# Feed-forward block products written as slots, each engine one step behind what it reads

## The chip, the cores and the metric

The kernel runs on one NeuronCore of one Trainium2 chip. The metric is the device time in microseconds (us) from start to end of one execution; where several runs are compared, their median.

## The reference

One decoder layer over 1024 tokens of width 1024: adaLN modulation, a mixer (sparse top-k attention of 8 heads beside a causal pooling), a LayerNorm, a SwiGLU feed-forward part of width 2816, a second LayerNorm. The change touches the feed-forward part alone:

```python
def swiglu(h, w_gate, w_up, w_down):
    return (jax.nn.silu(h @ w_gate) * (h @ w_up)) @ w_down
...
        h = x * (1.0 + scale2) + shift2
        ffn = swiglu(h, w_gate[l], w_up[l], w_down[l])
        x = layer_norm(ALPHA * x + gate2 * ffn, ln2_g[l], ln2_b[l])
```

## The kernel before

**Precision and splitting.** Every float32 operand of a matmul is kept as a high half (the value rounded to fp32r, written by ScalarE, ACT) and a low half (value less high half, a subtraction on VectorE, DVE, or GpSimd, POOL). A product of two blocks is then three matmuls: high by high, high by low, low by high.

**Tiling.** The 2816 feed-forward channels are cut into 11 pairs of 128-channel blocks (`NFP`), p = 0 to 10. For a pair the gate product, the up product and the down product are each a 2x2 by 2x2 block product done with seven block multiplications instead of eight (Strassen's scheme in Winograd's form). A **step** is one of the seven: 12 matmuls of 128x128 by 128x512 on TensorE (PE). I call the gate steps G1 to G7, the up steps U1 to U7 and the down steps D1 to D7, in the order of the tables `STEPS` and `DOWN`. G and U steps read the weight blocks A11, S3, S2, A12, S1, S4, A22 in that order, D steps the blocks B11, B21, T1, T4, T3, B22, T2. The names with S and T are sums or differences of quarters of the raw weights. Each D step also reads one block of activations: A11, A12, S1, A22, S3, S4, S2 for D1 to D7. In U the fourth step's twelve matmuls are halved, so that U4 has 6 and U5 has 18.

**Weights.** One megabyte of raw weights (four quarters of 128x512) is a set; two sets lie in SBUF (tiles `wraw_R` and `wraw_W`) and each is reloaded, on the SP queue, when its last block is made. POOL forms the sums and differences of quarters in place, for the down weights it first multiplies by the gate row `GR` ("gating", tile `gr`). ACT writes the block's high half, DVE (for down blocks POOL) its low half, into a ring of four blocks (tiles `wblk_V`, `wblk_T`). The function `make_block` issues all of this for one block at once, and `use_blocks` calls it after each step until `LEAD` = 4 blocks stand ahead of the next step.

**Results.** G and U steps accumulate in three PSUM banks (`gu`). G's results are combined on ACT and DVE and go through SiLU into `gtmp`; U's are combined in `utmp` and multiplied into `gtmp`. From the four products the seven activation blocks are made: A11, A12, A21 and A22 as they are or summed to S1, S2, S3, S4, each with a high half on ACT and a low half (tiles `act_W`, `act_R`). D steps go into four banks (`dn`), from which DVE adds into the residual stream (`res_X`), one addition of 128x512 per bank; the next D step writes the same four banks.

**Order.** From pair 1 on, the instructions of the four engines stay in the order in which the code issues them (`pinned`, through the `Queue` class); before and behind that a scheduler may move them. The table `DOWN_AT` interleaves a pair's G and U steps with the D steps of the pair before. Each step issues its matmuls, then its own combining, then the blocks to be made, then (`after_step`) low halves and sums put off from the step before. Every operation of all engines goes through the one helper that the profile shows as L159 (SP's as L156), so groups are told apart by their tiles.

The closing product (down weights of pairs 9 and 10, plain blocks), the residual and the second LayerNorm follow, 512 columns by 128 tokens at a time.

Of the kernel before, what the change touches and what calls it, by code (L numbers as in the profile page):

```python
# [171 lines left out]
def decoder_layer_kernel(  # L172
# [1149 lines left out]

    def make_block():
        if pos["made"] == len(blocks):
            return
        n_set, w_, end = blocks[pos["made"]]
        dst = block(pos["made"])
        pos["made"] += 1
        r = raw_set(n_set)
        a11, a12, a21, a22 = (r[:, q * 512 : (q + 1) * 512] for q in range(4))  # L1330
        if loads[n_set][0] == "d":
            gated = lambda x, c: G.tensor_tensor(x, x, GR[:, c * 512 : (c + 1) * 512], ALU.mult)
            if type(w_) is tuple:
                fi, c = w_
                src = r[:, fi * 1024 + c * 512 : fi * 1024 + (c + 1) * 512]
                gated(src, c)
            else:
                src = {"B11": a11, "B21": a21, "T1": a11, "T4": a21, "T3": a12, "B22": a22, "T2": a11}[w_]
                if w_ in ("B11", "B21"):
                    gated(src, 0)  # L1340
                elif w_ == "T1":
                    gated(a12, 1)
                    G.tensor_tensor(a11, a12, a11, ALU.subtract)
                elif w_ == "T4":
                    gated(a22, 1)
                    G.tensor_tensor(a11, a22, a11, ALU.subtract)
                    G.tensor_tensor(a21, a11, a21, ALU.subtract)
                elif w_ == "T3":
                    G.tensor_tensor(a12, a22, a12, ALU.subtract)
        else:  # L1350
            src = {"A11": a11, "S3": a11, "S2": a11, "A12": a12, "S1": a21, "A22": a22, "S4": a12}[w_]
            if w_ == "S3":
                G.tensor_tensor(a11, a11, a21, ALU.subtract)
            elif w_ == "S2":
                G.tensor_tensor(a11, a22, a11, ALU.subtract)
            elif w_ == "S1":
                G.tensor_tensor(a21, a21, a22, ALU.add)
            elif w_ == "S4":
                G.tensor_tensor(a12, a12, a11, ALU.subtract)
        split(dst, src, 512, G if loads[n_set][0] == "d" and type(w_) is str else V)  # L1360
        if end and n_set:
            load_set(n_set + 2)

    def use_blocks(n):
        pos["used"] += n

        lead = LEAD + 4 if pos["used"] >= len(blocks) - 11 else LEAD
        while pos["made"] < min(pos["used"] + lead, len(blocks)):
            make_block()

    def act_split(dst, s, j, eng):
        A.activation(dst[:, j], s[:, j], AF.Copy)
        eng.tensor_tensor(dst[:, 512 + j.start : 512 + j.stop], s[:, j], f_(dst[:, j]), ALU.subtract)

    gu_bank, gu_blk = {}, {}

    def gu_step(kind, n, i0, ni, act, halves=True):
# [18 lines left out]
        def out(q, val):

            s_ = GTMP[(0, 2, 1, 3)[q]]
            if kind == "g":
                A.activation(s_[:, j], val, AF.Silu)  # L1400
                return
            V.tensor_tensor(s_[:, j], s_[:, j], val, ALU.mult)
            if type(act) is list:
                act_split(act[q], s_, j, V)
                return
            g11, g12, g21, g22 = GTMP
            def act_hi(nm_, src):
                A.activation(act[nm_][:, j], src[:, j], AF.Copy)
                return lambda: (G if nm_ in ACT_G else V).tensor_tensor(
                    act[nm_][:, 512 + j.start : 512 + j.stop], src[:, j], f_(act[nm_][:, j]), ALU.subtract)  # L1410

            if q != 1:
                low.append(act_hi({0: "A11", 2: "A12", 3: "A22"}[q], s_))
            if q == 2:
                low.pop()()
            for nm_, dst, x, y, op in {1: (("S1", UTMP[0], g21, g22, ALU.add), ("S3", UTMP[2], g11, g21, ALU.subtract),
                                           ("S2", g11, UTMP[0], g11, ALU.subtract)),
                                       2: (("S4", g12, g11, g12, ALU.subtract),)}.get(q, ()):
                (G if nm_ in SUM_G else V).tensor_tensor(dst, x, y, op)
                if nm_ in SUM_G:  # L1420
# [265 lines left out]
```

## Time and profile before

| | |
|---|---|
| three runs | 1497.67, 1499.07, 1500.56 us; median 1499.07 |
| the profiled execution | 1506.66 us, of which the span of the profile is 1504.8 |
| TensorE, matmuls busy | 1267.5 us, 84% of the span |
| VectorE (DVE) busy | 1017.1 us, 68% |
| GpSimd (POOL) busy | 787.1 us, 52% |
| ScalarE (ACT) busy | 606.9 us, 40% |
| mean granted TensorE clock | 0.904 |

The span runs from the first to the last instruction; the execution's own time holds 1.9 us more, and profiled executions are timed apart from the three runs. Matmuls overlap, and a busy TensorE need not be at its full pace, so its share says little: how long a step of twelve takes says more. In the views, PE is TensorE's matmul queue and PEld its weight loads; a row `out<-in` names the tile written and those read; `[2.46 <-ACT gtmp_V]` is idle time ahead of the row and the instruction that ended it.

### The profile page before, as it was taken

The page shows a single profiled execution, that of the slowest core. Times are in us where ns is not written, and L with a number is a line of the kernel's source. Part 1 is how long each engine was busy: PE and PEld are TensorE (multiplying, and loading weights), DVE is VectorE, ACT ScalarE, POOL GpSimd, SP SyncE. Part 2 cuts the span into 40 slices and gives each one's busy share as a digit, 9 for nine tenths or more (in the row PEclk, how much of TensorE's full clock was granted, in tenths as well). Part 3 has the DMA queues.
Part 4 walks back from the last instruction along what each step waited for, and adds up shares of the span by engine and source line. Part 5 has one row for each costly group of instructions (what it writes and reads, how often), then busy time and mean ns, then how long its engine had stood idle before and what let it go on. Part 6 is the DMA issues. An engine that isn't in the chain of part 4 may idle for free.

```text
span 1504.8 us, 16018 instructions
## 1 busy us (share of the span) xinstructions
PE 1267.5 (84%) x5462; PEld 974.9 (65%) x5462; DVE 1017.1 (68%) x1740; ACT 606.9 (40%) x1141; POOL 787.1 (52%) x764
## 2 busy tenths in 40 slices
PE   7888978687699799966797979797979797979796
PEld 6655657565466458855675757575757575757675
DVE  6898898999877955885564646464646464646488
ACT  2456626446567662752232323232323232323331
POOL 1574856674243642466737373737373737272548
PEclk9999989897679989987898989898989898989998
DMA  9520113011003743011020202020202020202012
GB/s 346 208 99 15 53 39 112 29 42 35 14 15 107 237 157 124 1 42 42 28 84 0 84 0 84 1 84 0 84 1 84 1 84 0 84 0 84 28 56 112
DMA packets 24999, 101.80 MB, mean 68 GB/s; under 512 B 3411, under 2 KB 3411, under 8 KB 20566
## 3 DMA queue, kind: packets, MB, share of 16 engines
q1 hardware_dynamic: 24918, 100.78, 19.0%
q8 instruction: 43, 0.70, 0.2%
q14 instruction: 38, 0.31, 0.1%
HBM read 92.38 MB, written 8.40 MB: 67 GB/s over the span
## 4 chain that ended last, share of the span: by engine, by line
PE 21%; POOL 16%; DVE 6%; ACT 4%; issue 3%; DMA 1%; DVEq 0%; POOLq 0%; ACTq 0%; SPq 0%
PE gu L159 11%; PE dn L159 9%; POOL wraw_R L159 5%; POOL wraw_W L159 4%; POOL act_W L159 2%; POOL gtmp_V L159 2%; DVE act_W L159 1%; DVE gtmp_V L159 1%; ACT wblk_T L159 1%; ACT wblk_V L159 1%; POOL wblk_T L159 1%; POOL wblk_V L159 1%; DVE utmp_X L159 1%; ACT act_W L159 1%; POOL res_X L159 1%
## 5 line engine op out<-in xcount | busy, mean ns | idle before, releaser
L159 PE MATMUL gu<-hr_H,wblk_V 128*128 128x512 f32 (+1 forms) x936 | 229.1, 397 | 28.7 <-ACT gtmp_V L159 16.7
L159 PE MATMUL gu<-hr_H,wblk_T 128*128 128x512 f32 (+1 forms) x924 | 228.3, 402 | 23.3 <-ACT gtmp_V L159 20.1
L159 PEld LDWEIGHTS gu<-hr_H,wblk_V 128*128 128x128 f32 x936 | 180.3, 197 | 69.8 <-ACT gtmp_V L159 20.0
L159 PEld LDWEIGHTS gu<-hr_H,wblk_T 128*128 128x128 f32 x924 | 180.5, 201 | 63.8 <-ACT gtmp_V L159 23.6
L159 DVE TENSOR_TENSOR res_X<-res_X,dn 128x512 f32<-128x512 f32 (+1 forms) x253 | 156.9, 676 | 1.8 <-PE dn L159 1.8
L159 POOL TENSOR_TENSOR wraw_R<-wraw_R 128x512 f32<-128x512 f32 x64 | 86.1, 1348 | 107.6 <-DVE wblk_V L159 57.0
L159 PE MATMUL pj<-ws_W,hT_H 128*128 128x512 f32 x456 | 125.9, 426 | 18.9 <-DVE kr_K L159 6.5
L159 POOL TENSOR_TENSOR wraw_W<-wraw_W 128x512 f32<-128x512 f32 x60 | 79.3, 1326 | 92.1 <-DVE wblk_T L159 51.3
L159 PEld LDWEIGHTS pj<-ws_W,hT_H 128*128 128x128 f32 x456 | 89.8, 203 | 47.0 <-issue 16.8
L159 PE MATMUL dn<-wblk_T,act_W 128*128 128x512 f32 x324 | 94.8, 447 | 23.7 <-ACT wblk_T L159 14.3
L159 PE MATMUL dn<-wblk_V,act_W 128*128 128x512 f32 x324 | 94.7, 447 | 22.8 <-ACT wblk_V L159 14.3
L159 PEld LDWEIGHTS dn<-wblk_T,act_W 128*128 128x128 f32 x324 | 69.3, 217 | 45.4 <-ACT wblk_T L159 16.0
L159 PEld LDWEIGHTS dn<-wblk_V,act_W 128*128 128x128 f32 x324 | 69.4, 217 | 43.9 <-ACT wblk_V L159 16.0
L159 POOL TENSOR_SCALAR sm_H<-sm_H,stat_X 128x1024 f32<-128x1024 f32 (+7 forms) x64 | 58.4, 925 | 75.2 <-DVE stat_X L159 62.1
L159 DVE TENSOR_TENSOR wblk_V<-wraw_W,wblk_V 128x512 fp32r<-128x512 f32 x40 | 32.4, 810 | 78.0 <-ACT wblk_V L159 78.0
L159 DVE TENSOR_TENSOR wblk_V<-wraw_R,wblk_V 128x512 fp32r<-128x512 f32 x38 | 30.4, 800 | 80.7 <-ACT wblk_V L159 77.7
L159 DVE TENSOR_TENSOR wblk_T<-wraw_W,wblk_T 128x512 fp32r<-128x512 f32 x41 | 32.9, 805 | 76.8 <-ACT wblk_T L159 76.8
L159 DVE TENSOR_SCALAR_CACHE_REDUCE junk_X<-keysD_T,colsD_X 128x1024 int16<-128x1024 int16 (+1 forms) x64 | 79.0, 1270 | 0.8
L159 ACT ACTIVATE wblk_V<-wraw_R 128x512 fp32r<-128x512 f32 x56 | 35.1, 628 | 97.5 <-POOL wraw_R L159 71.0
L159 DVE TENSOR_TENSOR wblk_T<-wraw_R,wblk_T 128x512 fp32r<-128x512 f32 x36 | 28.8, 805 | 64.2 <-ACT wblk_T L159 64.1
L159 ACT ACTIVATE wblk_V<-wraw_W 128x512 fp32r<-128x512 f32 x54 | 33.9, 627 | 79.3 <-POOL wraw_W L159 63.3
L159 ACT ACTIVATE wblk_T<-wraw_W 128x512 fp32r<-128x512 f32 x55 | 34.3, 625 | 74.6 <-POOL wraw_W L159 60.0
(299 smaller groups left out, 2814.8 us busy)
## 6 DMA issues: line engine op xcount, KB each, us to landing
wm_K<-in_wma_dram SPq DMA_DIRECT2D x16, 512.0 KB, 8.9
modraw_V<-in_wmc_dram SPq DMA_DIRECT2D x16, 512.0 KB, 4.4
wraw_R<-in_wg_dram SPq DMA_DIRECT2D x6, 1024.0 KB, 4.8
wraw_R<-in_wd_dram SPq DMA_DIRECT2D x6, 1024.0 KB, 4.7
wraw_W<-in_wup_dram SPq DMA_DIRECT2D x6, 1024.0 KB, 4.7
modraw_V<-in_wmg_dram SPq DMA_DIRECT2D x10, 512.0 KB, 4.5
wraw_R<-in_wup_dram SPq DMA_DIRECT2D x5, 1024.0 KB, 4.8
wraw_W<-in_wg_dram SPq DMA_DIRECT2D x5, 1024.0 KB, 4.9
```

The costliest lines, as they stand in the source:

```text
L159: ins_ = f(*a, **k)
```

## The change

The steps' arithmetic is the same, and so are the matmuls of each. Four things differ.

1. **Slots.** `gu_step` and `down_step` issue only their matmuls and return a `Slot` with four parts: `copy` (ACT's copy of the step's own bank, or the four residual additions of a D step), `vec` (DVE's combining), `sums`, and `act` (ACT's SiLU or high halves of activations). `slot(sl)` then issues, behind the matmuls of this step: the `vec` of the step before, the low halves whose high halves were issued a slot ago, the `sums` of the step before, POOL's preparation, up to two high halves of weights, pending high halves of activations, the `act` of the step before, and last this step's `copy`.
2. **Weights.** `make_block` is cut into `block_prep` (POOL's sums and gating), `block_high` (ACT) and `block_low` (DVE or POOL). High halves reach up to `may_make()`, preparation one block further, as far as `may_prep()` finds that no quarter is overwritten that a later low half reads. Two halves of a set are reloaded apart: one behind S4's low half, one behind the last block's.
3. **Order.** `DOWN_AT` is new: a pair now runs G1 G2 D1 G3 D2 G4 G5 D3 G6 G7 D4 D5 U1 D6 U2 U3 D7 U4 U5 U6 U7, where it ran G1 G2 D1 G3 D2 G4 D3 G5 D4 G6 D5 G7 D6 U1 D7 U2 to U7.
4. **Who does what.** Only S4's low half of the activations and the sum S3 stay on POOL; the low halves of S2 and S3 and the sums S2 and S4 are on DVE. Before the last pair, POOL's eight additions on the residual stream stood in a row; now they stand behind single steps of that pair. Pair 0's G steps and their blocks are issued `at_once`, as before.

```diff
-LEAD = 4
-ACT_G = ("S2", "S3", "S4")
-SUM_G = ("S2", "S3", "S4")
-DOWN_AT = "ggdgdgdgdgdgduduuuuuu"
+ACT_G = ("S4",)
+DOWN_AT = "ggdgdggdggdduduuduuuu"
...
+    def block_prep():
+        n = pos["prep"]
+        pos["prep"] += 1
+        for st in steps_of(n):
+            if type(st) is int:
+                x = quad(n, st)
+                G.tensor_tensor(x, x, GR[:, st % 2 * 512 : (st % 2 + 1) * 512], ALU.mult)
+            else:
+                G.tensor_tensor(quad(n, st[0]), quad(n, st[1]), quad(n, st[2]), getattr(ALU, st[3]))
+
+    def block_high():
+        n = pos["made"]
+        pos["made"] += 1
+        A.activation(block(n)[:, 0:512], quad(n, from_of(n)), AF.Copy)
+
+    def block_low():
+        n = pos["low"]
+        pos["low"] += 1
+        n_set, w_, end = blocks[n]
+        by = G if loads[n_set][0] == "d" and type(w_) is str else V
+        by.tensor_tensor(block(n)[:, 512:1024], quad(n, from_of(n)), f_(block(n)[:, 0:512]), ALU.subtract)
+        if n_set and w_ == "S4":
+            load_set(n_set + 2, 0)
+        if n_set and end:
+            load_set(n_set + 2, 1 if loads[n_set][0] != "d" else None)
...
+    def may_prep():
+        n = pos["prep"]
+        if n == len(blocks):
+            return False
+        outs = {st if type(st) is int else st[0] for st in steps_of(n)}
+        return not any(blocks[m][0] == blocks[n][0] and from_of(m) in outs for m in range(pos["low"], n)) \
+            and all(blocks[m][0] != blocks[n][0] - 2 for m in range(pos["low"], n))
+
+    def may_make():
+        return min(len(blocks), pos["used"] + NRING + (4 if pos["used"] >= len(blocks) - 11 else 0))
...
+        def sums():
+            if kind == "u" and type(act) is dict:
+                g11, g12, g21, g22 = GTMP
+                todo_ = {5: (("S3", UTMP[2], g11, g21),), 6: (("S2", UTMP[0], UTMP[0], g11), ("S4", UTMP[1], UTMP[0], g12))}.get(n, ())
+                for nm_, dst, x, y in todo_:
+                    (G if nm_ == "S3" else V).tensor_tensor(dst, x, y, ALU.subtract)
+                    pend_high.append(lambda nm_=nm_, dst=dst: high(nm_, dst))
...
+    def slot(sl):
+        prev, last_slot[0] = last_slot[0], sl
+        prev.vec()
+        lows, pend_low[:] = list(pend_low), []
+        highs, pend_high[:] = list(pend_high), []
+        all_low()
+        for f in lows:
+            f()
+        prev.sums()
+        while pos["prep"] <= may_make() and may_prep():
+            block_prep()
+        for _ in range(min(2, may_make() - pos["made"])):
+            if pos["prep"] == pos["made"]:
+                if not may_prep():
+                    all_low()
+                block_prep()
+            block_high()
+        for f in highs:
+            f()
+        prev.act()
+        sl.copy()
+        pos["used"] += sl.used
```

Two places show what the rules make of the queues, both at the boundary from the first full pair to the next. On DVE, before, from S1's low half (`act_R`) and the combining of U7's bank to the first residual addition of D1 (`res_X`):

```order
L159 TENSOR_TENSOR act_R_4107<-utmp_X_4114,act_R_4107 128x512
L159 TENSOR_TENSOR utmp_X_4115<-utmp_X_4115,gu_5538 128x512
L159 TENSOR_TENSOR gtmp_V_4111<-gtmp_V_4111,utmp_X_4115 128x512
L159 TENSOR_TENSOR act_W_4105<-gtmp_V_4111,act_W_4105 128x512
L159 TENSOR_TENSOR wblk_T_4097<-wraw_R_4101,wblk_T_4097 128x512
L159 TENSOR_TENSOR wblk_V_4095<-wraw_R_4101,wblk_V_4095 128x512
L159 TENSOR_TENSOR res_X_4080<-res_X_4080,dn_5688 128x512
```

The same stretch now, from the combining of U7's bank; `act_W_4109` is S3, `act_W_4105` A12, `act_W_4108` S2, and the writes to `utmp_X_4114` and `utmp_X_4115` are the sums S2 and S4:

```order
L157 TENSOR_TENSOR utmp_X_4115<-utmp_X_4115,gu_5513 128x512
L157 TENSOR_TENSOR gtmp_V_4111<-gtmp_V_4111,utmp_X_4115 128x512
L157 TENSOR_TENSOR act_R_4107<-utmp_X_4114,act_R_4107 128x512
L157 TENSOR_TENSOR utmp_X_4114<-utmp_X_4114,gtmp_V_4110 128x512
L157 TENSOR_TENSOR utmp_X_4115<-utmp_X_4114,gtmp_V_4111 128x512
L157 TENSOR_TENSOR wblk_T_4097<-wraw_R_4101,wblk_T_4097 128x512
L157 TENSOR_TENSOR act_W_4109<-utmp_X_4116,act_W_4109 128x512
L157 TENSOR_TENSOR act_W_4105<-gtmp_V_4111,act_W_4105 128x512
L157 TENSOR_TENSOR act_W_4108<-utmp_X_4114,act_W_4108 128x512
L157 TENSOR_TENSOR res_X_4080<-res_X_4080,dn_5686 128x512
```

Two sums and two low halves have come into this stretch of DVE's queue, ahead of D1's additions; one of two low halves of weights (`wblk`) has gone behind them.

On POOL, before, from the sum S3 (`utmp_X_4116`) on; `wraw_W` holds the down weights, `gr_G` is the gate row, and `act` rows are low halves of activations:

```order
L159 TENSOR_TENSOR utmp_X_4116<-gtmp_V_4110,gtmp_V_4112 128x512
L159 TENSOR_TENSOR gtmp_V_4110<-utmp_X_4114,gtmp_V_4110 128x512
L159 TENSOR_TENSOR wraw_W_4102<-wraw_W_4102,gr_G_76 128x512
L159 TENSOR_TENSOR wblk_T_4096<-wraw_W_4102,wblk_T_4096 128x512
L159 TENSOR_TENSOR gtmp_V_4111<-gtmp_V_4110,gtmp_V_4111 128x512
L159 TENSOR_TENSOR wraw_R_4101<-wraw_R_4101 128x512
L159 TENSOR_TENSOR act_W_4109<-utmp_X_4116,act_W_4109 128x512
L159 TENSOR_TENSOR act_W_4108<-gtmp_V_4110,act_W_4108 128x512
L159 TENSOR_TENSOR wraw_W_4102<-wraw_W_4102,gr_G_76 128x512
L159 TENSOR_TENSOR wblk_V_4094<-wraw_W_4102,wblk_V_4094 128x512
```

And now:

```order
L157 TENSOR_TENSOR utmp_X_4116<-gtmp_V_4110,gtmp_V_4112 128x512
L157 TENSOR_TENSOR wraw_W_4102<-wraw_W_4102,gr_G_76 128x512
L157 TENSOR_TENSOR wraw_R_4101<-wraw_R_4101 128x512
L157 TENSOR_TENSOR wblk_T_4096<-wraw_W_4102,wblk_T_4096 128x512
L157 TENSOR_TENSOR wraw_W_4102<-wraw_W_4102,gr_G_76 128x512
L157 TENSOR_TENSOR wblk_V_4094<-wraw_W_4102,wblk_V_4094 128x512
L157 TENSOR_TENSOR act_W_4104<-utmp_X_4115,act_W_4104 128x512
```

Between the gating of D1's block and the low half of D2's block (`wblk_V_4094`) stood six operations and stand now three; the sums S2 and S4 and the low halves of S3 and S2 are gone from this queue.

More of the change, by code (lines that the diff above doesn't have):

```diff
@@ L1316, in raw_set, with load_set @@
         return SETS[(n + 1) % 2 if n else 0]
-    def load_set(n):
+    def load_set(n, half=None):
         if n < len(loads):
             kind, p = loads[n]
-            SP.dma_start(raw_set(n), {"g": wg_in, "u": wup_in, "d": wd_in}[kind][p])
-    def make_block():
[L1324 to L1373, printed above, removed]
-    gu_bank, gu_blk = {}, {}
+            dst, src = raw_set(n), {"g": wg_in, "u": wup_in, "d": wd_in}[kind][p]
@@ L1392, in mm @@
                              start=(new and k == 0 and m == 0), stop=(k == 3 and m == 2), skip_group_check=True)
+        mm(ps_, n, range(2 if n == 3 and halves else 4), n in (0, 1, 3))
+        if n == 4 and halves:
+            mm(banks["B"], 3, (2, 3), False)
         t1, t2, t4 = (x[:, j] for x in ((GTMP[0], GTMP[1], GTMP[3]) if kind == "g" else UTMP))
[L1396 to L1420, printed above, removed]
-                    low2.append(lambda nm_=nm_, dst=dst: act_hi(nm_, dst)())
-                else:
-                    low.append(act_hi(nm_, dst))
@@ new lines, in gu_step, with copy, vec @@
+        sl = Slot()
+        sl.used = ((1, 1, 1, 0, 2, 1, 1)[n] if halves else 1) if i0 + ni == 4 else 0
+        def copy():
+            if n in (0, 2, 4):
+                A.activation((t1, None, t2, None, t4)[n], ps_, AF.Copy)
+        def vec():
+            for q, val in outs:
+                if n == 4:
+                    V.tensor_tensor(val, val, banks["D" if q == 3 else "B"], ALU.add)
+                elif n == 6:
+                    V.tensor_tensor(val, val, ps_, ALU.add)
+                if kind == "u":
+                    V.tensor_tensor(place(q)[:, j], place(q)[:, j], val, ALU.mult)
+            if kind == "u" and n == 5 and type(act) is dict:
+                V.tensor_tensor(UTMP[0], place(1), place(3), ALU.add)
@@ new lines, in act_ @@
+        def act_():
+            for q, val in outs:
+                if kind == "g":
+                    A.activation(place(q)[:, j], val, AF.Silu)
+                elif type(act) is list:
+                    high(q, place(q))
+                elif q == 1:
+                    high("S1", UTMP[0])
+                else:
+                    high({0: "A11", 2: "A12", 3: "A22"}[q], place(q))
+        sl.copy, sl.vec, sl.sums, sl.act = copy, vec, sums, act_
+        return sl
+    pend_low, pend_high = [], []
@@ L1538, in decoder_layer_kernel @@
     for n in range(7):
-        gu_step("g", n, 2, 2, None)
+        at_once(gu_step("g", n, 2, 2, None))
         if n in (1, 3, 5, 6):
             affine()
-    gate_up("u", ACTS, lambda n: affine())
+    for n in range(7):
+        slot(gu_step("u", n, 0, 4, ACTS))
+        affine()
     pairs.close()
```

125 lines of the change are left out of this document (74 added, 51 removed).

## The prediction

> **What bounds the kernel now.** I read the busy time by engine first, then TensorE's timeline through the pairs of the feed-forward part, then the timelines of the engines that TensorE waits for. In the page's first part no engine is full over the span:
>
> ```profile
> PE 1267.5 (84%) x5462; PEld 974.9 (65%) x5462; DVE 1017.1 (68%) x1740; ACT 606.9 (40%) x1141; POOL 787.1 (52%) x764
> ```
>
> TensorE's timeline from the first pair's end, one row per run of matmuls (start, length, engine, out<-in, count, idle time ahead and what ended it). From 802.58 to the last row is one whole pair, first down-projection step (dn) to first down-projection step:
>
> ```profile
> 729.05 2.88 PE L159 MATMUL dn<-wblk_V,act_W 128*128 128x512 f32 x12
> ...
> 802.58 0.79 PE L159 MATMUL dn<-wblk_T,act_W 128*128 128x512 f32 x1 [3.57 <-ACT wblk_T L159]
> 803.93 5.06 PE L159 MATMUL dn<-wblk_T,act_W 128*128 128x512 f32 x11 [0.56 <-POOL wblk_T L159]
> 811.45 4.61 PE L159 MATMUL gu<-hr_H,wblk_T 128*128 128x512 f32 x12 [2.46 <-ACT gtmp_V L159]
> 815.89 2.90 PE L159 MATMUL dn<-wblk_V,act_W 128*128 128x512 f32 x12
> ...
> 824.12 2.97 PE L159 MATMUL dn<-wblk_T,act_R 128*128 128x512 f32 x12 [2.60 <-DVE res_X L159]
> ...
> 831.70 4.43 PE L159 MATMUL dn<-wblk_V,act_W 128*128 128x512 f32 x12 [1.89 <-ACT gtmp_V L159]
> ...
> 866.02 5.60 PE L159 MATMUL gu<-hr_H,wblk_V 128*128 128x512 f32 x24
> 871.47 2.88 PE L159 MATMUL gu<-hr_H,wblk_T 128*128 128x512 f32 x12
> 877.91 0.80 PE L159 MATMUL dn<-wblk_T,act_W 128*128 128x512 f32 x1 [3.57 <-ACT wblk_T L159]
> ```
>
> Undisturbed, 24 matmuls take 871.47-866.02 = 5.45 us, so a step of 12 takes 2.72 and the 21 steps of a pair 57.1. The pair took 877.91-802.58 = 75.3. Of the 18.2 us over, 11.1 are the five idle times shown (3.57+0.56+2.46+2.60+1.89), and some 6 are the same matmuls at a lower pace behind such a gap: 4.44 from 811.45 to 815.89 where 2.72 would do. All the loss lies in the first ten steps after the boundary of two pairs; the last eleven run dense. What is late there stands on POOL and ACT:
>
> ```profile
> 872.06 1.80 POOL L159 TENSOR_TENSOR utmp_X<-gtmp_V,gtmp_V 128x512 f32<-128x512 f32 x1 [3.27 <-DVE gtmp_V L159]
> 873.94 1.59 POOL L159 TENSOR_TENSOR gtmp_V<-utmp_X,gtmp_V 128x512 f32<-128x512 f32 x1
> 875.49 1.71 POOL L159 TENSOR_TENSOR wraw_R<-wraw_R,gr_G 128x512 f32<-128x512 f32 x1
> ```
>
> ```profile
> 877.23 0.63 ACT L159 ACTIVATE wblk_T<-wraw_R 128x512 fp32r<-128x512 f32 x1 [3.86 <-POOL wraw_R L159]
> ```
>
> The gating of the first down-projection weight stands behind two sums of activations, so ACT writes that block's high half at 877.23, and TensorE, free since 874.3, starts at 877.91. The pairs run from 729.05 to the last pair's d0 at 1328.61, eight of them in 599.6 us, and 115.3 us later the closing matmuls begin:
>
> ```profile
> 1328.61 0.80 PE L159 MATMUL dn<-wblk_V,act_W 128*128 128x512 f32 x1 [3.57 <-ACT wblk_V L159]
> ...
> 1443.94 0.39 PE L159 MATMUL dn<-hr_H,act_R 128*128 128x512 f32 x1
> ```
>
> **The change, part by part.** *Order of the steps, and what each queue does in a step.* A block of weights still goes into a ring of four, so its high half can be written one step after its buffer's last reader in both kernels; new is that its low half follows a step later, that POOL's preparation runs a block further ahead, and that the activations' tail (two sums and two low halves) moves from POOL to DVE. Per pair DVE then has 26 operations with two SBUF operands (14 low halves of weights, 6 of activations, 3 products, 3 sums) where it had 22, and 35 with a PSUM operand as before; POOL has 25 (12 differences, 4 gatings, 7+1 low halves, 1 sum) where it had 29. Their prices:
>
> ```profile
> L159 DVE TENSOR_TENSOR res_X<-res_X,dn 128x512 f32<-128x512 f32 x232 | 143.3, 678 | 0.0
> L159 POOL TENSOR_TENSOR wraw_W<-wraw_W 128x512 f32<-128x512 f32 x52 | 68.2, 1316 | 78.6 <-DVE wblk_T L159 39.1 <-DVE wblk_V L159 38.5
> L159 ACT ACTIVATE wblk_V<-wraw_R 128x512 fp32r<-128x512 f32 x47 | 29.4, 626 | 74.3 <-POOL wraw_R L159 63.6 <-PE gu L159 3.7 <-PE dn L159 3.6
> L159 DVE TENSOR_TENSOR wblk_T<-wraw_W,wblk_T 128x512 fp32r<-128x512 f32 x33 | 25.2, 764 | 67.5 <-ACT wblk_T L159 67.5
> ```
>
> 143.3/232 = 0.62 us is the pace of DVE's additions in a row, 25.2/33 = 0.76 that of a low half; POOL's differences are 1.31. So DVE needs 26x0.76+35x0.62 = 41.5 us of a pair, POOL 25x1.31 = 32.8, ACT 38x0.63 = 23.9 (21 high halves, 17 copies, silus and activations). All lie under 57.1: no engine but TensorE is full, and TensorE's own work is unchanged. What decides is whether the chain across the boundary comes in time.
>
> *The boundary, laid out by hand.* DVE's price there depends on POOL. From the same boundary of the first pair, DVE and POOL:
>
> ```profile
> 720.69 0.68 DVE L159 TENSOR_TENSOR gtmp_V<-gtmp_V,utmp_X 128x512 f32<-128x512 f32 x1
> 721.29 1.77 DVE L159 TENSOR_TENSOR act_W<-gtmp_V,act_W 128x512 fp32r<-128x512 f32 x1
> ...
> 725.89 1.78 DVE L159 TENSOR_TENSOR utmp_X<-gtmp_V,gtmp_V 128x512 f32<-128x512 f32 x1
> ```
>
> ```profile
> 720.85 1.67 POOL L159 TENSOR_TENSOR wraw_W<-wraw_W 128x512 f32<-128x512 f32 x1 [0.63 <-DVE wblk_T L159]
> ...
> 725.38 1.74 POOL L159 TENSOR_TENSOR wblk_V<-wraw_R,wblk_V 128x512 fp32r<-128x512 f32 x1
> 727.08 1.74 POOL L159 TENSOR_TENSOR wraw_W<-wraw_W 128x512 f32<-128x512 f32 x1
> 728.78 1.29 POOL L159 TENSOR_TENSOR act_W<-utmp_X,act_W 128x512 fp32r<-128x512 f32 x1
> ```
>
> A two-SBUF operation of DVE that meets one of POOL ends 0.55 us after POOL's (723.06 against 722.52; 727.67 against 727.12), and a row of both advances by one of each in 1.70 (725.38, 727.08, 728.78). I take 1.70 for each such meeting. The Trainium skill, SBUF — State Buffer, Who interferes with whom, says that such a pair excludes each other wholly: the second "fully blocks". By it a meeting costs the whole of both, 0.68+1.29 = 1.97, and the eight meetings below 2.2 us a pair more, 20 in all; the 1.70 here is shorter, and the sum goes by it.
>
> Now the new order, in us from the start of step U6 (up, sixth); dense, TensorE would start U7 at 2.72, G1 5.44, G2 8.16, D1 10.88, G3 13.60, D2 16.32, G4 19.04. DVE ends the four operations on U5's result at 2.2 (in the old trace too they start 0.5 before U6), and the low half of G1's block at 2.8. That frees POOL, which then has six operations without a pause: G2's difference to 4.1, the sum S3 5.8, D1's gating 7.5, G3's difference 9.2, D1's low half 10.9, D2's gating 12.6. Against them stand DVE's: sum S1 4.6, G2's low half 6.3, A22's low half 8.0, A11's 9.7, U7's addition from PSUM 10.4, its product 11.4, S1's low half 13.1, sum S2 13.75. ACT gets D2's gated block at 12.6, so POOL's low half of D2 runs from 13.3 to 15.0 and holds DVE's sum S4 to 15.5; G3's low half is done at 16.1. G1, G2 and D1 find all they need. **G3 waits 2.5**, from 13.60. Then the low halves of S3 16.7, A12 18.4, S2 20.1, and D1's first addition 20.7: it frees the bank that D2 writes, so **D2 waits 1.9**, from 18.85; the other banks follow at 0.62 against TensorE's 0.68. G4's low half (23.2) is ahead of G4 (23.5). From there to the next U5 DVE has at most 4.5 us in a step (D3: two additions, a low half, four additions) with steps of nothing behind it, and I find no wait. Sum 4.4 us.
>
> *The clock behind these waits.* After 2.60 idle a step took 2.81 (824.12), after 1.89 it took 4.22 (831.70 to the next at 835.92): between 0.1 and 1.5 us, and if G3 is the slow one it is hidden in D2's wait. I take 0.9 a pair. The Trainium skill, TensorE: Matmul & The Clock Gate, HAM oscillation, has the clock drop only for idle gaps over about 3.4 us. By it this term is nothing and the time 8 us lower; the step behind 1.89 speaks against that.
>
> *Waits that are added.* ACT's copy of a step's bank now stands last in its slot: behind it wait the next step's high halves, whose low halves follow a step and whose reader three steps later, so the cover is about a step, 2.7 us; without it that much would fall on TensorE. A D step's four additions stand last on DVE: behind them wait low halves read two steps later. *Loads.* Each up load, and each down load, is issued as two halves when half a buffer is free. The worst landing of half a megabyte in the trace:
>
> ```profile
> raw_R<-in_wiq_dram SPq DMA_DIRECT2D x4, 512.0 KB, 10.6
> ```
>
> The up weights' first half is issued behind G6's low half (28.0 by the same reckoning) and its block is read by U1 at 42.6: with 10.6 it lands at 38.6, so both edits cost nothing. SP has no other load queued between them. *The residual additions on POOL*, eight at once before the last pair, are spread over it: POOL has then at most two other operations in a step, and I count nothing for them beyond the last pair's term below.
>
> **The sum**, against the profiled execution (1506.7, span 1504.8): a pair takes 57.1+4.4+0.9 = 62.4. Eight pairs: 499.2 for 599.6, saves 100.4. From the last d0 to the closing matmuls: 19 steps 51.7, the waits 5.3, the last pair's 14 steps 38.1 and 2 for its own boundary (an estimate from the 4.4, without a down step) are 97.1 for 115.3, saves 18.2. What lies ahead of 729 and behind the closing matmuls stays. 1506.7-118.6 = 1388.1. The runs' median, 1499.07, lies 7.6 under the profiled execution; I take this off: **1380.5 us**. Runs lie 3 us apart, so 0.2% is about what a measurement can tell from no change.
>
> **Rivals.** *The boundary comes out clean* (chance 0.20): POOL and DVE meet less than I laid out. With DVE at 0.62 and POOL at 1.29 throughout, the same ledger has G3's low half done at 10.6, three us early. Then 57.1 a pair: 142.8 and 25.5 saved, 1330.8. For it: only about one in ten of the low halves meets POOL now (0.76 is little over 0.69). Against: POOL's six operations in a row.
>
> *DVE is the bound* (0.22): if every two-SBUF operation meets POOL, a pair needs 26x1.70+35x0.62 = 65.9 on DVE. Eight pairs save 72.4; the end takes 59.6+38.1+4 and saves 13.6: 1413. Against it: POOL is busy only 32.8 of 62.
>
> *Slower: the clock never recovers* (0.05). Where the waits fall in many steps rather than two, each step costs the 4.44 of the row at 811.45, 1.72 more. From (75.3-62.4)/1.72 = 7.5 steps of 21 on the change loses. With all 21 a pair takes 93.2: 146 more over eight pairs, and 33 steps at 4.44 = 146.5 at the end for 115.3, 31 more: 1499.07+177 = 1676. Against: steps 11 to 21 already run dense.
>
> *The change doesn't do what it says* (0.03): the down blocks' gating is still late because POOL's preparation waits on low halves; it stays over 1425 or unchanged (0.01 within 0.2%).
>
> **How the numbers follow.** The forecast has 0.50, the four cases above 0.20, 0.22, 0.05 and 0.03. The range goes from the clean boundary less its 0.2%, 1328, to DVE as the bound with 0.5 us of lost clock a pair, 1418; it leaves out the slower case, the last, and some of the edges, under 0.2. Faster 0.94, same 0.01, slower 0.05.
>
> **What would show it.** Right: d0 to d0 in 61 to 64 us, idle time of TensorE ahead of G3 by a DVE low half (wblk) and ahead of D2 by DVE's residual addition, no idle ahead of D1, and DVE's low halves near 1.7 at the boundary. Wrong: idle time ended by ACT or POOL, gaps in steps 11 to 21, or steps over 4 us outside the boundary.

## The result and the profile after

The changed kernel takes 1372.07 us (median of four runs, 1370.75 to 1373.61); runs of the kernel before on the same chip took 1499.36. The ratio is 0.9152, with an interval of 0.9136 to 0.9168. The profiled execution took 1373.61, its span 1371.8. Of the page, the busy times and a load of down weights:

```profile
PE 1208.7 (88%) x5462; PEld 939.4 (68%) x5462; DVE 1095.5 (80%) x1776; ACT 605.7 (44%) x1141; POOL 769.6 (56%) x728
...
wraw_R<-in_wd_dram SPq DMA_DIRECT2D x12, 512.0 KB, 3.6
```

TensorE has the same 5462 matmuls and is busy 59 us less; the mean granted clock is 0.944 where it was 0.904. DVE is busier by 78. TensorE's timeline from one D1 to the next, and on to G4:

```profile
786.16 3.07 PE L157 MATMUL dn<-wblk_T,act_W 128*128 128x512 f32 x12
790.08 3.19 PE L157 MATMUL gu<-hr_H,wblk_T 128*128 128x512 f32 x12 [0.85 <-ACT gtmp_V L157]
795.37 3.00 PE L157 MATMUL dn<-wblk_V,act_W 128*128 128x512 f32 x12 [2.11 <-DVE res_X L157]
...
836.29 2.88 PE L157 MATMUL gu<-hr_H,wblk_T 128*128 128x512 f32 x12
...
847.17 3.00 PE L157 MATMUL dn<-wblk_T,act_W 128*128 128x512 f32 x12
851.06 3.18 PE L157 MATMUL gu<-hr_H,wblk_V 128*128 128x512 f32 x12 [0.90 <-ACT gtmp_V L157]
856.35 3.00 PE L157 MATMUL dn<-wblk_V,act_W 128*128 128x512 f32 x12 [2.11 <-DVE res_X L157]
859.19 5.60 PE L157 MATMUL gu<-hr_H,wblk_T 128*128 128x512 f32 x24
```

847.17-786.16 = 61.0 us, and over eight pairs (first D1 726.06, ninth 1214.80) 61.09 on average, where it was 74.9. Nothing waits ahead of D1 now. Two idle times are left, ahead of G3 and of D2. By the starts, D1 to G3 is 3.89, G3 to D2 5.29 and D2 to G4 2.84 where 2.72 would do: 3.9 us. The other steps run dense, but for D2's own matmuls, which run slow behind the gap in two of nine pairs (last section). What DVE does at this boundary:

```profile
842.69 3.47 DVE L157 TENSOR_TENSOR act_W<-gtmp_V,act_W 128x512 fp32r<-128x512 f32 x2
...
847.79 1.78 DVE L157 TENSOR_TENSOR act_R<-utmp_X,act_R 128x512 fp32r<-128x512 f32 x1
849.61 1.42 DVE L157 TENSOR_TENSOR utmp_X<-utmp_X,gtmp_V 128x512 f32<-128x512 f32 x2
850.94 0.69 DVE L157 TENSOR_TENSOR wblk_V<-wraw_W,wblk_V 128x512 fp32r<-128x512 f32 x1
...
852.14 1.78 DVE L157 TENSOR_TENSOR act_W<-gtmp_V,act_W 128x512 fp32r<-128x512 f32 x1
853.85 1.75 DVE L157 TENSOR_TENSOR act_W<-utmp_X,act_W 128x512 fp32r<-128x512 f32 x1
855.53 2.47 DVE L157 TENSOR_TENSOR res_X<-res_X,dn 128x512 f32<-128x512 f32 x4
```

It never pauses from the low halves of A22 and A11 (842.69) to D1's four additions (855.53), and D2 starts 0.2 behind the end of the first of these (0.62 long, a quarter of the row). ACT over the same time:

```profile
850.41 0.60 ACT L157 ACTIVATE gtmp_V<-gu 128x512 f32<-128x512 f32 x1 [1.88 <-DVE utmp_X L157]
850.91 0.62 ACT L157 ACTIVATE wblk_V<-wraw_R 128x512 fp32r<-128x512 f32 x1
```

The first row is the copy of G1's bank. It writes the buffer of g11, which DVE's sum S2 (849.61) still reads, so ACT stands for 1.88 us and G3, which accumulates on the copied bank, starts at 851.06. The second is the high half of D2's block, queued behind it.

The end of the last pair, where U6 waits for ACT and runs slow behind it:

```profile
1300.15 5.60 PE L157 MATMUL gu<-hr_H,wblk_T 128*128 128x512 f32 x24
1308.41 7.33 PE L157 MATMUL gu<-hr_H,wblk_V 128*128 128x512 f32 x24 [2.66 <-ACT utmp_X L157]
1315.58 0.84 PE L157 MATMUL dn<-hr_H,act_R 128*128 128x512 f32 x3
```

### The profile page after: what moved, and what is told of

The parts are those of the page before. It is cut to its first block, busy times and chain, and to the rows that moved or that the text cites. A ratio compares the mean times of both kernels' runs of the same rounds, so it can differ in the third digit from the quotient of the medians.

```text
span 1371.8 us, 15996 instructions
## 1 busy us (share of the span) xinstructions
PE 1208.7 (88%) x5462; PEld 939.4 (68%) x5462; DVE 1095.5 (80%) x1776; ACT 605.7 (44%) x1141; POOL 769.6 (56%) x728
## 4 chain that ended last, share of the span: by engine, by line
PE 39%; DVE 38%; POOL 8%; issue 6%; ACT 5%; DMA 2%; SPq 0%; DVEq 0%; POOLq 0%; ACTq 0%
PE gu L157 17%; PE dn L157 14%; DVE junk_X L157 7%; DVE act_W L157 5%; DVE score_X L157 3%; DVE utmp_X L157 2%; PE o L157 2%; POOL res_X L157 2%; DVE stat_C L157 2%; PE pT L157 2%; PE s L157 2%; DVE res_X L157 2%; POOL colsA_X L157 1%; DVE gtmp_V L157 1%; DVE wblk_V L157 1%
## 5 line engine op out<-in xcount | busy, mean ns | idle before, releaser
L157 PE MATMUL gu<-hr_H,wblk_T 128*128 128x512 f32 (+1 forms) x912 | 216.0, 390 | 6.2 <-ACT gtmp_V L157 3.5
L157 PEld LDWEIGHTS gu<-hr_H,wblk_T 128*128 128x128 f32 x912 | 170.2, 193 | 43.6 <-ACT gtmp_V L157 6.0
L157 POOL TENSOR_TENSOR wraw_W<-wraw_W 128x512 f32<-128x512 f32 x60 | 87.7, 1465 | 96.7 <-DVE wblk_T L157 40.8
L157 PE MATMUL dn<-wblk_T,act_W 128*128 128x512 f32 x324 | 81.8, 404 | 10.6 <-DVE res_X L157 10.6
L157 PE MATMUL dn<-wblk_V,act_W 128*128 128x512 f32 x324 | 78.5, 392 | 8.4 <-DVE res_X L157 8.4
L157 PEld LDWEIGHTS dn<-wblk_V,act_W 128*128 128x128 f32 x324 | 60.2, 188 | 23.4 <-issue 10.0
L157 DVE TENSOR_TENSOR gtmp_V<-gtmp_V,gu 128x512 f32<-128x512 f32 (+1 forms) x47 | 29.9, 652 | 57.4 <-PE gu L157 29.4
L157 ACT ACTIVATE wblk_T<-wraw_R 128x512 fp32r<-128x512 f32 x54 | 33.8, 630 | 64.2 <-POOL wraw_R L157 34.9
L157 POOL TENSOR_TENSOR colsA_X<-colsA_X 128x1 f32<-128x1 f32 (+1 forms) x124 | 33.4, 278 | 49.4 <-ACT junkA_T L157 38.9
L157 POOL TENSOR_TENSOR ws_W<-raw_R,ws_W 128x1024 fp32r<-128x1024 f32 x11 | 29.9, 2721 | 51.0 <-ACT ws_W L157 51.0
```

Source lines behind the costliest of these rows:

```text
L157: ins_ = f(*a, **k)
```

## The experiments

Each kernel ran beside runs of the kernel before, and ratios refer to these (1499 to 1502 us). "D1 to D1" is the mean of eight pairs in the profile; "the tail" is the sums S2 and S4 and the low halves of S2 and S3.

| kernel | ratio to before | us | D1 to D1 |
|---|---|---|---|
| before | 1 | 1499.36 | 74.94 |
| the change | 0.9152 (0.9136 to 0.9168) | 1372.07 | 61.09 |
| old order in the change | 0.9184 (0.9160 to 0.9209) | 1378.7 | 62.15 |
| tail on POOL in the change | 0.9145 (0.9120 to 0.9170) | 1372.38 | 61.50 |
| no lead in the change | 0.9162 (0.9135 to 0.9190) | 1374.76 | 61.65 |
| these three undone: slots only | 0.9518 (0.9493 to 0.9543) | 1428.68 | 67.56 |
| new order in the kernel before | 0.9681 (0.9650 to 0.9712) | 1452.32 | 69.61 |
| tail on DVE in the kernel before | 0.9803 (0.9782 to 0.9824) | 1471.3 | 71.44 |
| low halves of S3, S2 held | 0.8964 (0.8942 to 0.8985) | 1346.17 | 58.53 |
| G1's copy in its own buffer | 0.9109 (0.9090 to 0.9128) | 1367.05 | 60.61 |
| all held | 0.9009 (0.8986 to 0.9031) | 1351.7 | 59.10 |
| D1's and D2's gating left out | 0.8984 (0.8966 to 0.9002) | 1348.53 | 58.82 |
| order kept to the end | 0.9122 (0.9106 to 0.9139) | 1369.43 | 61.47 |
| all held, mended, order kept | 0.8925 (0.8908 to 0.8943) | 1339.8 | 58.17 |

### Where the gain came from: one part undone, one part alone

**Old order in the changed kernel.**

```diff
-DOWN_AT = "ggdgdggdggdduduuduuuu"
+DOWN_AT = "ggdgdgdgdgdgduduuuuuu"
```

> The changed kernel with the steps of a pair in the old order (G1 G2 D1 G3 D2 G4 D3 G5 D4 G6 D5 G7 D6 U1 D7 U2 to U7); the slots and the lead of the preparation stay. Theory A, the slots carry the gain: the first five steps are the same in both orders, so the boundary's waits stay near 3 us a pair; behind them D3 has one step of G between it and D2 instead of two, and may wait up to 2 us. 61.1 us a pair becomes 61 to 63.5: 1372 to 1392 us. Rival B, the order carries it: the waits of 2.60 and 1.89 and the slow steps behind them that the kernel before had in its sixth to tenth steps (about 6 us a pair) come back: 1415 us or more.

1378.7 us, as theory A has it: G3's 0.9 and D2's 2.1 stay, no wait comes ahead of D3, and a POOL low half ends one of 0.36 ahead of D4. With the slots in place the order is worth 5 to 7 us. In the profiles some 3 of these are two more slow steps behind D2's gap (four of nine pairs instead of two), and no run shows that the order makes them.

**New order in the kernel before**, the mirror (old line for new):

> The kernel before with the new order of the steps alone; its blocks are made as before. Theory A: G1 G2 D1 G3 D2 come in the same order, so the waits ahead of D1 (3.57 and 0.56) and G3 (2.46) and the slow step behind them stay; at most the later two (2.60 and 1.89, with their slow steps up to 7.5 us a pair) go: 1440 to 1490 us of 1499. Rival B, the order carries the gain: 1415 us or less.

1452.32 us, again A. TensorE at one of its boundaries:

```profile
861.48 0.51 PE L159 MATMUL dn<-wblk_T,act_W 128*128 128x512 f32 x1 [3.62 <-ACT wblk_T L159]
862.83 4.38 PE L159 MATMUL dn<-wblk_T,act_W 128*128 128x512 f32 x11 [0.85 <-POOL wblk_T L159]
870.34 4.36 PE L159 MATMUL gu<-hr_H,wblk_V 128*128 128x512 f32 x12 [3.13 <-ACT gtmp_V L159]
```

The waits ahead of D1 and G3 are those of before, or somewhat longer (3.13 for 2.46); of the later two, 0.5 to 1.0 us ahead of D5 is left. Alone the order gains some 48 us, in the slots 6.

**Tail on POOL in the changed kernel.**

```diff
-ACT_G = ("S4",)
+ACT_G = ("S2", "S3", "S4")
...
-                    (G if nm_ == "S3" else V).tensor_tensor(dst, x, y, ALU.subtract)
+                    G.tensor_tensor(dst, x, y, ALU.subtract)
```

> The changed kernel with the sums S2 and S4 and the low halves of S2 and S3 on POOL, as before; slots, order and lead stay. Theory A, that who does the tail matters: POOL gets four more operations of 1.3 to 1.7 us between the boundary and G5, 5 to 7 us, in front of gatings and differences that its lead can cover by one step, 2.7 us: 2 to 4 us a pair more, 1390 to 1405 us. Rival B, that only D2's wait for DVE counts there: DVE has four operations fewer ahead of D1's additions, D2's wait of 2.1 goes and nothing takes its place: 1352 to 1360 us.

1372.38 us: no change, and neither theory. Each had half of it:

```profile
853.16 0.50 PE L157 MATMUL dn<-wblk_V,act_W 128*128 128x512 f32 x1
854.98 2.81 PE L157 MATMUL dn<-wblk_V,act_W 128*128 128x512 f32 x11 [1.31 <-POOL wblk_V L157]
...
863.37 0.39 PE L157 MATMUL dn<-wblk_V,act_R 128*128 128x512 f32 x1
864.62 2.79 PE L157 MATMUL dn<-wblk_V,act_R 128*128 128x512 f32 x11 [0.86 <-POOL wblk_V L157]
```

D2's wait for DVE's addition is gone, as B says; POOL's low halves are late for D2 (1.31) and D3 (0.86) in its place, as A says, and the two are about equal. The pairs are 0.4 us longer (61.50); in the profiles the start and the stretch behind the ninth D1, shorter by 2.0 and 2.3, hide that.

**No lead in the changed kernel.**

```diff
-        while pos["prep"] <= may_make() and may_prep():
-            block_prep()
```

> The changed kernel without POOL's lead: a block's difference or gating is issued in the slot that writes its high half, not one ahead. Theory A: the high half is written three steps ahead of its reader, so outside the boundary the cover of 5 us holds; at the boundary D1's gating falls behind the sum S3 and the difference of G2, about one operation of 1.7 us later, of which D1 had 0 to 1 to spare: 0 to 2 us a pair, 1372 to 1390 us. Rival B, the lead is what removed D1's wait: 3.6 us a pair and a slow step come back, 1400 to 1415 us.

1374.76 us, within A and hardly apart from the change; the same two waits stand at the boundary, and one of 0.39 is new ahead of D5.

**The tail on DVE in the kernel before.**

```diff
-ACT_G = ("S2", "S3", "S4")
-SUM_G = ("S2", "S3", "S4")
+ACT_G = ("S4",)
+SUM_G = ("S3",)
```

> The kernel before with the sums S2 and S4 and the low halves of S2 and S3 on DVE instead of POOL, as in the changed kernel; no slots, no lead, old order. It takes from POOL the sum S2 that stands ahead of the gating of D1's weights and 5 us of other work behind it. Theory A, what carries the gain is that D1's weights are not queued behind the last pair's tail: D1's 3.6 us fall by about 1.6, its 0.6 for POOL and some of G3's 2.5 go too, 2 to 5 us in each of nine pairs: 1455 to 1482 us. Rival B, it is who does the tail: most of the gain comes with this edit, 1400 us or less. Rival C, DVE is late instead, and the wait only changes its releaser: 1490 to 1505 us.

1471.3 us, A. D1's wait falls from 3.57 to 2.53 with the sum S2 out of POOL's queue, and G3's 2.46 falls to 0.8 or nothing. D2 now waits for DVE's additions, 1.5 to 1.8 us; the two later waits stay:

```profile
935.14 0.53 PE L159 MATMUL dn<-wblk_V,act_W 128*128 128x512 f32 x1 [2.53 <-ACT wblk_V L159]
...
946.45 2.96 PE L159 MATMUL dn<-wblk_T,act_W 128*128 128x512 f32 x12 [1.48 <-DVE res_X L159]
954.02 2.97 PE L159 MATMUL dn<-wblk_V,act_R 128*128 128x512 f32 x12 [1.89 <-DVE res_X L159]
961.58 4.41 PE L159 MATMUL dn<-wblk_T,act_W 128*128 128x512 f32 x12 [1.87 <-ACT gtmp_V L159]
```

**Slots only**: the three edits to the changed kernel together.

> The changed kernel with three of its parts undone together: the old order of the steps, the sums S2 and S4 and the low halves of S2 and S3 on POOL, and no lead of the preparation. What is left of the change are the slots: each block's high half, low half and the activations' tail queued one step apart, and the halved loads. Undone alone the three parts cost 6.6, 0 and 2.7 us. Theory A, the slots carry the gain because they put the gating of D1's weights ahead of the tail's sums in POOL's queue, whoever has the lead: the three add up, 1376 to 1395 us. Rival B, the parts stand in for each other and one of them is needed: 1415 us or more.

1428.68 us: rival B. Undone singly the parts cost 6.6, 0.3 and 2.7 us by the medians (4.8, -1.0 and 1.5 by the ratios), together 56.6 (54.9). TensorE at the boundary, then POOL and ACT:

```profile
862.08 2.88 PE L157 MATMUL dn<-wblk_T,act_W 128*128 128x512 f32 x12
868.44 5.49 PE L157 MATMUL gu<-hr_H,wblk_V 128*128 128x512 f32 x12 [3.48 <-ACT gtmp_V L157]
```

```profile
862.32 2.66 POOL L157 TENSOR_TENSOR utmp_X<-utmp_X,gtmp_V 128x512 f32<-128x512 f32 x2 [1.23 <-DVE act_R L157]
864.94 1.26 POOL L157 TENSOR_TENSOR wraw_W<-wraw_W 128x512 f32<-128x512 f32 x1
```

```profile
866.23 0.63 ACT L157 ACTIVATE wblk_V<-wraw_W 128x512 fp32r<-128x512 f32 x1 [6.26 <-POOL wraw_W L157]
...
867.81 0.58 ACT L157 ACTIVATE gtmp_V<-gu 128x512 f32<-128x512 f32 x1
```

D1 comes in time with the slots alone; so far A is right. But the two sums then stand ahead of G3's difference (864.94), ACT waits 6.26 us for that, G1's copy (867.81) stands behind, and G3 waits 3.48. G3's matmuls run slow behind it (5.28 us, granted clock 0.50), and some 3 us more a pair are short waits for ACT and POOL ahead of D3, D4 and G6. Either the lead (the difference goes ahead of the sums) or the tail on DVE (the sums leave the queue) cures G3's wait: it is 0.75 with the tail on POOL and 0.90 without the lead. Both of these kernels have the new order; what each does alone with the old one was not run.

### The two waits that are left

**Low halves of S3 and S2 held back.**

```diff
+        if prev.dn == 1:
+            pend_low.extend(held)
+            held.clear()
...
-            pend_low.append(...
+            (held if nm_ in ("S3", "S2") else pend_low).append(...
```

> The changed kernel with DVE's low halves of S3 and S2 (read at D5 and D7) held back behind the residual additions of D1 and D2; nothing else moves. Theory A, D2's wait of 2.1 us is DVE's queue: the two low halves of 1.7 us ahead of D1's first addition are gone, so the addition comes 3.4 us earlier and D2 starts when G3 is through. 2.1 us in each of nine pairs, 19 us: 1350 to 1356 us; TensorE's only wait left at the boundary is G3's 0.9. Rival B, the wait moves on: D2 waits for its own block (POOL's low half) or G4 for its low half, behind the two that were held: 1362 to 1372 us.

1346.17 us: A's mechanism, and more than its number. D2's wait is gone and G3's stays:

```profile
844.42 3.19 PE L157 MATMUL gu<-hr_H,wblk_V 128*128 128x512 f32 x12 [0.90 <-ACT gtmp_V L157]
847.45 2.88 PE L157 MATMUL dn<-wblk_V,act_W 128*128 128x512 f32 x12
```

In the profiles 1371.8-1345.3 = 26.5 us: eight pairs 20.5, the stretch behind the ninth D1 4.0, the start 1.9. A's 19 counted nine gaps of 2.1. Of the other 7.5, 3.2 are two slow steps that the change had behind such gaps (last section) and this kernel hasn't, 1.9 the start, and the rest some 0.3 a pair by which the steps beside a gap run longer.

**G1's copy in its own buffer.**

```diff
+    GT1 = buf("W", 6144, 512, "gtmp")
...
-        t1, t2, t4 = (x[:, j] for x in ((GTMP[0], GTMP[1], GTMP[3]) if kind == "g" else UTMP))
+        t1, t2, t4 = (x[:, j] for x in ((GTMP[0] if ni < 4 else GT1, GTMP[1], GTMP[3]) if kind == "g" else UTMP))
...
-                    pend_high.append(lambda nm_=nm_, dst=dst: high(nm_, dst))
+                    (late if nm_ == "S2" else pend_high).append(lambda nm_=nm_, dst=dst: high(nm_, dst))
```

> The changed kernel with ACT's copy of G1's bank in a buffer of its own (that of S2's high half, which is made later for it), so that the copy no longer waits for the sum S2 that reads the old one. Theory A: the copy ended G3's wait only because it came last; G3's own low half ends 0.6 us behind it, behind the same sums on DVE, so G3 starts at most 0.3 earlier and D2 still waits for D1's additions: 1369 to 1373 us. Rival B, the copy is the wait: 0.9 us in each of nine pairs, 1362 to 1365 us.

1367.05 us, between the two. A is right that G3's low half on DVE is the next limit, but not how far:

```profile
786.17 3.02 PE L157 MATMUL dn<-wblk_T,act_W 128*128 128x512 f32 x12
789.02 0.61 PE L157 MATMUL gu<-hr_H,wblk_T 128*128 128x512 f32 x2
791.65 2.56 PE L157 MATMUL gu<-hr_H,wblk_T 128*128 128x512 f32 x10 [2.01 <-DVE wblk_T L157]
794.64 2.98 PE L157 MATMUL dn<-wblk_V,act_W 128*128 128x512 f32 x12 [0.44 <-DVE res_X L157]
```

```profile
788.62 2.37 DVE L157 TENSOR_TENSOR utmp_X<-utmp_X,gtmp_V 128x512 f32<-128x512 f32 x2
790.91 0.68 DVE L157 TENSOR_TENSOR wblk_T<-wraw_R,wblk_T 128x512 fp32r<-128x512 f32 x1
```

G3 starts at once, runs two matmuls on the high half, and its third waits 2.01 for the low half. With ACT free, POOL has D2's low half already at 788.78 and it meets DVE's sums: the pair of them takes 2.37 where the change had 1.42. What was gained came at D2, because the low half of S2, whose high half this kernel makes later, no longer stands ahead of D1's additions. Part of the gain went to the clock: in five of eight pairs G3's ten matmuls behind the 2.01 to 2.04 run slow (3.5 to 4.2 us where others took 2.6; granted clock 0.57 in one of them), and such a pair takes 61.2 instead of 60.2.

**All held**: both edits, and S1's low half and the sums S2 and S4 behind D1's additions.

> Both of the edits before (low halves of S3 and S2 held back, G1's copy in a buffer of its own), and the low half of S1 and the sums S2 and S4 (read at D3, D7 and D6) also held behind D1's residual additions. Theory A, the boundary's waits are DVE's queue and nothing else: G3's low half and D1's additions find DVE free, both waits go, up to 3.9 us in each of nine pairs with 0 to 0.5 left: 1335 to 1342 us. Rival B, three engines carry the chain: POOL's six operations, up to 12.7 us behind U6, hold D2's block and then G4's, and half or more of the 3.9 stays as a wait for POOL: 1352 us or more.

1351.7 us: both expectations missed, and it is slower than holding two low halves. G3 and D2 find all they need, but two new waits stand further on:

```profile
797.72 3.06 PE L157 MATMUL gu<-hr_H,wblk_T 128*128 128x512 f32 x12 [0.66 <-ACT gtmp_V L157]
...
812.27 3.00 PE L157 MATMUL dn<-wblk_T,act_W 128*128 128x512 f32 x12 [0.61 <-DVE res_X L157]
```

In the next pair the sums now run from 852.75 to 856.11 and ACT's copy of G3's bank, which overwrites g12, starts at 856.23; G5 needs that bank. (The profile names G4's matmuls, which end at the same time, as what released the copy. In the change the same copy, at 857.31, comes ahead of G4, at 859.19, so it doesn't need them.) D5 waits for D4's additions, which stand behind S2's low half. The wait moved to where the held work went, and not to POOL as B had it.

**D1's and D2's gating left out.**

```diff
-            "B11": (0,), "B21": (2,),
+            "B11": (), "B21": (),
```

> The changed kernel without the gating of D1's and D2's weights in the pairs (the first half column of their gate is left out of the result); POOL has two of the six operations fewer that it does in a row at the boundary. Theory A, DVE's low halves take 1.7 us there because each meets one of POOL: with two meetings fewer DVE is 1.6 to 2 us earlier at D1's additions, and D2's wait falls from 2.1 to 0.1 to 0.5: 1356 to 1360 us. Rival B, DVE's length there is its own (the number of its operations): its rows keep their 1.7 and D2's wait its 2.1: 1370 to 1374 us.

1348.53 us: A's mechanism, with a time under its range. DVE's rows at the same place as in the change, and POOL's beside the first:

```profile
837.44 2.38 DVE L157 TENSOR_TENSOR act_W<-gtmp_V,act_W 128x512 fp32r<-128x512 f32 x2
...
841.45 0.68 DVE L157 TENSOR_TENSOR act_R<-utmp_X,act_R 128x512 fp32r<-128x512 f32 x1
```

```profile
837.60 1.67 POOL L157 TENSOR_TENSOR wraw_W<-wraw_W 128x512 f32<-128x512 f32 x1 [0.63 <-DVE wblk_T L157]
```

The same low halves take 2.38 instead of 3.47 and 0.68 instead of 1.78, 2.19 us less: the first two meet one of POOL's operations instead of two, and the third meets none. That two meetings went with exactly two of POOL's operations shows the cause. G3's wait vanishes and D2's falls to 1.42, not to A's 0.5, since G3 comes earlier too. What A's range lacks is mostly that no step runs slow here (3.2 us of slow steps in the change) and that the first D1 comes 1.9 earlier.

### The end, and a version with all of it

**Order kept to the end.**

```diff
-    pinned.clear()
     while last_slot[0].used or pend_low or pos["low"] < len(blocks):
         slot(Slot())
+    pinned.clear()
```

> The changed kernel with the order of the program kept on all engines through the trailing slots too (it was let go ahead of them). Theory A: in the last pair ACT's copy of U5's bank stands behind a high half of a closing block that waits 5.8 us for POOL's gating and that was let past it; kept in order, U6 loses its wait of 2.66 and the slow matmuls behind it (7.33 us for 24, 1.9 over): 4 to 5 us, 1366 to 1368.5 us. Rival B, the gatings are the limit there either way, and the closing matmuls wait for the blocks that now come later: 1371 to 1374 us.

1369.43 us, between the two. U6 has no wait, and U6 and U7 take 5.44 instead of 7.17, so the 4.4 us (2.66+1.73) are there; but the closing matmuls then wait 0.92 for a low half that comes later, and the stretch behind their start grows from 56.2 to 57.9.

**All held, mended, order kept.** The version with all held, with S1's low half ahead of D1's additions again, S2's low half behind D5's, and the order kept.

> The version with all held back (G1's copy in its own buffer, low half of S3 and the sums S2 and S4 behind D1's additions), mended where its own waits showed up: S1's low half ahead of D1's additions again, so that the sum S4 ends 1.8 us earlier and ACT's copy of G3's bank with it; S2's low half behind D5's additions instead of D3's; and the order kept through the trailing slots. Theory A, only what is due at once may stand ahead at the boundary: G3, D2, G5 and D5 find all they need and a pair takes 57.1 to 58: nine pairs save 3 to 3.9 each against 1372, and the end 4 to 5: 1331 to 1341 us. Rival B, the wait moves a third time, to where the held work now stands: not under the 1346 of the version with two low halves held.

1339.8 us, 0.8925 of before and 2.5% under the change: within A's range, at its upper end. Of the 33.2 us between the profiles, 23.4 are eight pairs, 8.9 the stretch behind the ninth D1 and 2.6 the start, which no edit touches; 1.7 are lost behind the closing matmuls' start. TensorE has one wait left in a pair (from its timeline):

```profile
850.93 3.03 PE L157 MATMUL gu<-hr_H,wblk_T 128*128 128x512 f32 x12 [0.68 <-ACT gtmp_V L157]
```

It is G5's again, for ACT's copy behind the sum S4: the two sums take 3.48 there, since each meets POOL. So one of the mends did nothing: S1's low half, moved ahead of D1's additions, put these back by as much, and S4 ends 11.1 us behind D1's start with it and without it. D5's wait is gone, and that and the order kept to the end are what this version gained on the one before, beside a start 4.1 us earlier.

## Why the prediction was right, and where it was not

**The sum.** 1380.5 was forecast and 1372.07 came. For the profiled execution it was 1388.1 and 1373.6, 14.5 less: pairs -10.5, the stretch behind the ninth D1 +3.7, ahead of the first -3.0, behind the closing matmuls' start -4.7. The offset to the median was 1.5, not 7.6, which gives 6.1 back. That is luck: the 7.6 came from one execution of the kernel before and did not repeat.

**What bounds it** held, and the ledger has D1's gating start at 5.8 us behind U6, where it came. But the prediction reads its lateness before as two sums ahead of it, and that is the smaller part. Counted from U6's start, the gating began at 12.2 before (875.49, U6 at 863.30) and begins at 5.9 now (842.17, U6 at 836.29). The sum S2, now behind it, is 1.6 of these 6.3 us. The sum S3 still stands ahead of it, but starts 4.6 earlier. The product that S3 reads was queued on DVE behind the low halves of two blocks, each of which waited for ACT's high half; now these come a step later and the product follows U6 at once. DVE before, DVE now, POOL now:

```profile
869.49 0.69 DVE L159 TENSOR_TENSOR wblk_T<-wraw_W,wblk_T 128x512 fp32r<-128x512 f32 x1 [2.06 <-ACT wblk_T L159]
...
871.30 0.68 DVE L159 TENSOR_TENSOR gtmp_V<-gtmp_V,gu 128x512 f32<-128x512 f32 x1
```

```profile
839.21 0.69 DVE L157 TENSOR_TENSOR gtmp_V<-gtmp_V,gu 128x512 f32<-128x512 f32 x1
```

```profile
840.47 1.74 POOL L157 TENSOR_TENSOR utmp_X<-gtmp_V,gtmp_V 128x512 f32<-128x512 f32 x1
842.17 1.74 POOL L157 TENSOR_TENSOR wraw_R<-wraw_R,gr_G 128x512 f32<-128x512 f32 x1
```

Two kernels separate the parts. With the tail on DVE in the kernel before, S2 is gone from the queue, S3 starts as late as ever and D1 still waits 2.53; in slots only, S3 starts 4.1 behind U6 and D1 doesn't wait. The text also gave the gain to the whole list of edits without saying that they cover for each other: three of them are worth almost nothing singly and 57 us together.

**D2's wait** was right in place and cause: DVE's queue ahead of D1's first addition. Counted from U6's start (836.29) that addition was to end at 20.7 and D2 started at 20.06.

**G3's wait failed as a step.** The prediction has "ACT gets D2's gated block at 12.6, so POOL's low half of D2 runs from 13.3 to 15.0 and holds DVE's sum S4 to 15.5; G3's low half is done at 16.1". ACT was not free at 12.6: it stood at G1's copy until 14.1, for a buffer that the sum S2 still read. So POOL's low half came late, S4 was not held, G3's low half was done at 15.3, and G3 started at 14.8, 1.2 late (0.9 of it idle) instead of 2.5. In the kernel with the copy in its own buffer the step comes true: counted from its U6 (775.29), S4 ends at 15.7 and G3's low half at 16.3. The order of the queues had been followed, but not which operand an instruction overwrites. "Idle time ended by ACT" was one of the prediction's own signs of being wrong, and G3's idle time is that. The sum hardly felt it, because DVE's queue sets D2's start whatever G3 does: D2 was to come 4.4 late (20.7 for 16.3) and came 3.7 late.

**1.70 us for a meeting** of DVE and POOL held: where both have work in a row, each advances by 1.67 to 1.73 (POOL from 840.47 to 847.29 and from 851.61 to 856.70), and leaving out two gatings takes 2.19 us from DVE. By the Trainium skill, SBUF — State Buffer, Who interferes with whom, the two exclude each other. The rows bear out that they take turns; the full price that this rule would give for both in a row, 0.68+1.29 = 1.97, is longer than the pitch measured.

**The clock** was over-priced: 0.9 us a pair, against one slow step of 1.6 over in eight pairs, 0.2. The rule of the Trainium skill (TensorE: Matmul & The Clock Gate, HAM oscillation), that gaps over about 3.4 us are what to avoid, would have had 0, nearer in sum; but it leaves no place for a gap of 2.1 us that slows the clock, and here some do (last section).

**Waits that are added.** "ACT's copy of a step's bank now stands last in its slot" was covered by "about a step", and counted at nothing. That copy is what ends the waits of G3, of U6 in the last pair, and of G5 in two experiments. At U6 it stood behind a closing block's high half which the scheduler, let free for the trailing slots, had put ahead of it; this made the last stretch 100.8 instead of 97.1, together with a slow step.

**What stays.** The halved loads land in 3.6 us and no engine waits for them (before, ACT waited 1.6 to 3.5 us in each pair for a load of up weights). The start differs with no edit there: the first D1 comes between 722 and 729 us in the fourteen profiles. Differences of 2 or 3 us between two kernels, as for the tail or the lead undone singly, can't be put down to their edits. The end was not unchanged: before, the closing matmuls had waited 1.65 and 0.73 for low halves and run slow behind; now they start dense.

**Rivals.** A boundary without waits ahead of G3 and D2 exists, but takes other edits: 58.2 us a pair. DVE as the bound is refuted: the windows of single pairs have it busy 47.4 us of 61, though that is more than the 41.5 forecast (POOL 37.1 for 32.8). A clock that never recovers did not show.

## What to carry to other kernels

At a boundary where several engines hand over, sort each queue by when its result is read, not by when its operands are ready: holding back two low halves that nobody needed yet was worth over 20 us, and holding back too much made a new wait. Look at what an instruction overwrites as closely as at what it reads, since a copy into a buffer that is still read stops all that is queued behind it. And before an edit is judged by undoing it alone, undo its companions too: parts that cover for each other all look worthless singly.
